# A two-layer encoder trunk on one core: folding neighbour blocks in mixer A, and moving q's transposes in mixer B

## The chip, the cores and the metric

The kernel runs on one core of a Trainium2 chip. The metric is the device time of one execution in microseconds (us). Five engines work side by side, each on its own list of instructions in order: TensorE (PE; its weight loads are PEld in the profile), VectorE (DVE), ScalarE (ACT), GpSimd (POOL) and SyncE (SP, which here only issues DMAs). TensorE writes to PSUM; the other memory on the core is SBUF.

## The reference

A sequence of 1024 tokens of width 1024, seen as a grid of 16 rows and 64 columns, goes through two layers. Layer 0 uses mixer A, layer 1 mixer B; each is followed by an output projection, a residual add and a gated embedding (`ple`).

```python
def mixer_a(h, w_in, rpb, w_out):          # 16 heads of 64
    q, k, v, gate = split(h @ w_in)
    # each query sees a clamped window of 8 rows x 16 columns of keys
    sc = einsum(q, k[window]) * scale + rpb[offset]
    o = einsum(softmax(sc), v[window])
    return (o * silu(gate)) @ w_out

def mixer_b(h, w_in, q_norm_g, k_norm_g, w_out):   # 16 q heads, 4 k/v heads
    q, k, v, gate = split(h @ w_in)
    q, k = rope(rms_norm(q)), rope(rms_norm(k))
    o = einsum(softmax(einsum(q, k) * scale), v)     # all 1024 keys
    return (o * silu(gate)) @ w_out

for i in range(2):
    x = x + mixer[i](rms_norm(x), ...)
    x = x + sigmoid(rms_norm(x) @ w_gate) * (p[i] @ w_proj)
return rms_norm(x)
```

All inputs are float32.

## The kernel before

**Tokens and blocks.** The tokens are laid out in 8 blocks of 128: block j holds the grid's columns 8j to 8j+7, all 16 rows. A window of 16 columns around a query of block j then lies in blocks j-1, j and j+1. Of block j-1 it takes the columns whose place in the block is at or after the query's, of block j+1 those before it. Blocks 0 and 7 are edges: the clamped window lies in two blocks there.

**Products.** Every float32 operand of a projection is split into a high and a low part (`HTh`/`HTl`, `wh`/`wl`, `PTh`/`PTl`), and the products are added up in PSUM. `mm` (line 317) issues every matmul of projections, scores and v products, so the profile tells these apart by tile names: `d` is a projection ("dense"), `s` scores, `o` products of probabilities with v, `t` transposes.

**Mixer A** (lines 655 to 998) goes through 128 steps (head h, block j). `f_S` computes the scores of one query block against its two or three key blocks (256 or 384 columns, L317 into `s`), and one DVE instruction (L754) adds the table `TB` of position biases and masks and takes the row minimum (the scores are negated). `f_E` (L763) is the exponential with its row sum. `f_T` transposes each block of 128 columns (L771), copies them to the high part (ACT, L774) and subtracts to get the low part (DVE, L775). `f_AV` multiplies one key block of v with the transposed probabilities of its two or three query blocks. `head_end` ends each half of a head: copy (L532), join (L496), reciprocals, and for each pair of heads the denominators go out to DRAM and come back spread over the partitions (`rb`, L503 and L505); then POOL multiplies `Y` by the gate `G` (L576) and by `rb` (L577), called four steps later. POOL also builds the table of the next head (`table`, L729, called at j = 1) and issues accumulating DMAs (L645, one a step while the list lasts).

**The order is written out by hand.** At step n of mixer A the program issues the small jobs (`head`), the transposes of step n, the exponential of step n+1, the scores of step n+2 and the v products of step n-2. `mix` strews the dense pieces (the next head's q and k, gates) between these items by weight. After each item `pulse` splits a weight unit when one is due and counts down the postponed pieces in `post`, so `QD = (2, 5, 8)` means that many items later.

**q and k of mixer A.** `qk_evac` takes a projected half head out of PSUM and makes `QS`, `KA` and `KB`, each with a part in both halves of the partitions: two ACT copies (L698, L699), two DVE subtractions (L702, L703), and two DVE copies of k's parts to the other half (L704, L707).

**Mixer B** (lines 1000 to 1326) runs 128 steps (head pair, half, head, 128 queries) in the same manner, with 1024 keys: scores into a two-bank PSUM tile (`psS`), minimum (L1211), exponential (L1217), eight transposes (`f_T`, L1227) into two buffers of `psT`, copies and subtractions (L1229, L1230), and `f_AV` for two query blocks at a time: eight products with the high part, then eight with the low. Once in 8 steps `q_stack` transposes the next q (L1181) into a `psT` buffer, and ACT copies it out (L1183). It stands in a queue called `after`, which `mix` runs behind the next dense piece. PSUM has eight banks: mixer B's pools are opened in the order `pd` (1), `psS` (4), `psT` (2), `psO` (1); the first projections alternate between `pd` and `psO`.

**The dense phases** (`dense_phase`, lines 1507 to 1729) follow each mixer. In the last one POOL multiplies X by the final norm's gain (L1706); the program puts these behind the test `n >= 17`, which counts dense pieces.

## Time and profile before

| | |
|---|---|
| median of 3 runs | 1526.33 us (1525.96 to 1526.63) |
| profiled execution, its own time | 1525.28 us |
| span of its profile | 1523.4 us |
| PE busy | 1496.9 us, 98% |
| DVE busy | 1096.4 us, 72% |
| ACT busy | 899.8 us, 59% |
| POOL busy | 303.8 us, 20% |
| attention loop of mixer A | about 57 to 530 us of the span |
| dense phase 0 | about 530 to 710 us |
| mixer B, start and loop | about 710 to 1338 us |
| dense phase 1 | about 1338 us to the end |

A row of the profile gives line, engine, operation, output<-inputs, sizes and count, then busy time in us, the mean of one in ns, and the idle time of the engine just before with what ended it. A row of a timeline gives start, duration, engine, line and operation; "x3" merges three in a row, and a bracket gives idle time before it and what ended that. The shown end of a matmul is modelled and overlaps the next one. Some matmul records are missing from the trace (352 transposes of L771 are shown, 368 are issued).

### The profile page before, as it was taken

What the parts mean: (1) busy time and instruction counts of PE and PEld (TensorE: products, weight loads), DVE (VectorE), ACT (ScalarE), POOL (GpSimd) and SP (SyncE); (2) the same over time, 40 slices, a digit from 0 to 9 for tenths busy, and PEclk for the clock granted to TensorE, in tenths of its full rate; (3) what the DMA queues carried; (4) which work ended last, traced back from release to release, by engine and by line L of the source; (5) the groups of instructions that cost most, each with busy time, mean ns of one, the idle gap of its engine ahead of it and who ended that gap; (6) DMA issues with size and microseconds to landing.
All of it is one profiled execution on the core that took longest, in us unless ns stands there. A gap on an engine that the chain in (4) does not pass through costs nothing.

```text
span 1523.4 us, 24376 instructions
## 1 busy us (share of the span) xinstructions
PE 1496.9 (98%) x8976; PEld 1314.9 (86%) x8976; DVE 1096.4 (72%) x2091; ACT 899.8 (59%) x1801; POOL 303.8 (20%) x413
## 2 busy tenths in 40 slices
PE   8999999999999999999999999999999999999997
PEld 8888988988988888888998999989999888878786
DVE  7566576377477599767888786777877777789856
ACT  6565465366466635443467776666767777744432
POOL 1222232133112000010222222443131300000022
PEclk9999999999999999999999999999999999999999
DMA  8325255263121963262210111111111122763123
GB/s 255 120 98 139 82 144 163 63 157 93 36 87 56 345 249 97 83 196 93 75 50 22 32 45 50 40 32 54 47 31 45 38 76 68 237 228 115 66 88 134
DMA packets 91096, 157.22 MB, mean 103 GB/s; under 512 B 18144, under 2 KB 54112, under 8 KB 90464
## 3 DMA queue, kind: packets, MB, share of 16 engines
q1 hardware_dynamic: 85824, 139.66, 27.9%
q0 software_dynamic: 2560, 8.39, 3.1%
q10 hardware_dynamic: 2592, 7.61, 1.4%
q8 instruction: 71, 1.16, 0.3%
q14 instruction: 49, 0.40, 0.1%
HBM read 125.10 MB, written 50.83 MB: 115 GB/s over the span
## 4 chain that ended last, share of the span: by engine, by line
PE 43%; DVE 6%; ACT 2%; issue 1%; DMA 0%; POOL 0%; ACTq 0%; DVEq 0%; POOLq 0%
PE d L317 19%; PE o L317 9%; PE s L317 7%; PE t L1227 7%; PE t L317 1%; DVE xn L1560 1%; DVE PTl L1230 1%; DVE X L1456 0%; PE t L1181 0%; DVE wl L231 0%; DVE mn L1211 0%; DVE HTl L482 0%; DVE HTl L1402 0%; ACT PTh L1229 0%; ACT th L1183 0%
## 5 line engine op out<-in xcount | busy, mean ns | idle before, releaser
L317 PE MATMUL d<-wh,HTh 128*128 128x256 f32 (+1 forms) x1032 | 342.5, 334 | 3.9 <-ACT HTh L481 1.6
L317 PE MATMUL d<-wh,HTl 128*128 128x256 f32 (+1 forms) x1032 | 338.0, 329 | 0.3 <-DVE HTl L482 0.3
L317 PE MATMUL d<-wl,HTh 128*128 128x256 f32 (+1 forms) x1032 | 336.7, 328 | 0.0
L1230 DVE TENSOR_TENSOR PTl<-t,PTh 128x512 fp32r<-128x512 f32 x256 | 165.1, 684 | 108.7 <-ACT PTh L1229 107.5
L317 PEld LDWEIGHTS d<-wh,HTh 128*128 128x128 f32 x1032 | 194.8, 190 | 24.5 <-ACT HTh L481 2.0
L317 PEld LDWEIGHTS d<-wl,HTh 128*128 128x128 f32 x1032 | 194.7, 190 | 19.3
L317 PEld LDWEIGHTS d<-wh,HTl 128*128 128x128 f32 x1032 | 194.9, 190 | 18.8 <-DVE HTl L482 0.5
L317 PE MATMUL d<-HTh,wh 128*128 128x512 f32 x504 | 205.2, 407 | 0.0
L317 PE MATMUL d<-HTh,wl 128*128 128x512 f32 x504 | 198.2, 393 | 0.0
L317 PE MATMUL d<-HTl,wh 128*128 128x512 f32 x504 | 197.3, 392 | 0.0
L1217 ACT ACTIVATE P<-s,mn 128x1024 f32<-128x1024 f32 x128 | 142.8, 1116 | 51.8 <-DVE mn L1211 50.9
L1229 ACT ACTIVATE PTh<-t 128x512 fp32r<-128x512 f32 x256 | 139.9, 594 | 52.8 <-PE t L1227 52.0
L1211 DVE TENSOR_REDUCE mn<-s 128x1 f32<-128x1024 f32 x128 | 154.7, 1209 | 11.2 <-PE s L317 11.0
L1227 PE MATMUL t<-ident,P 128*128 128x128 f32 x1024 | 136.4, 274 | 5.2 <-ACT th L1183 2.9
L317 PE MATMUL s<-KA,QS 128*128 128x512 f32 (+2 forms) x384 | 134.5, 404 | 0.0
L1227 PEld LDWEIGHTS t<-ident,P 128*128 128x128 f32 x1024 | 115.2, 140 | 16.6 <-DVE PTl L1230 6.7
L231 DVE TENSOR_TENSOR wl<-wstage,wh 128x1024 fp32r<-128x1024 f32 x78 | 100.3, 1290 | 34.9 <-ACT wh L226 34.4
L317 PE MATMUL s<-KB,QS 128*128 128x512 f32 (+2 forms) x384 | 121.6, 371 | 0.0
L775 DVE TENSOR_TENSOR PTl<-t,PTh 128x384 fp32r<-128x384 f32 (+1 forms) x128 | 66.6, 520 | 75.4 <-ACT PTh L774 74.0
L317 PE MATMUL o<-PTh,V 128*128 128x256 f32 (+2 forms) x672 | 118.5, 287 | 1.2 <-DVE Y L496 0.8
L317 PE MATMUL o<-PTl,V 128*128 128x256 f32 (+2 forms) x672 | 119.1, 288 | 0.7 <-DVE PTl L1230 0.6
L317 PEld LDWEIGHTS d<-HTh,wl 128*128 128x128 f32 x504 | 94.6, 188 | 21.7
(237 smaller groups left out, 2694.1 us busy)
## 6 DMA issues: line engine op xcount, KB each, us to landing
wstage<-in_wts SPq DMA_DIRECT2D x88, 512.0 KB
pp<-ppD SPq DMA_DIRECT2D x32, 256.0 KB
X<-in_x SPq DMA_DIRECT2D x15, 512.0 KB
rb<-rD SPq DMA_DIRECT2D x56, 128.0 KB
ppD<-th SPq DMA_DIRECT2D x20, 256.0 KB
tD0t<-in_wts SPq DMA_DIRECT2D x16, 256.0 KB
tD1t<-in_wts SPq DMA_DIRECT2D x16, 256.0 KB
xD<-X SPq DMA_DIRECT2D x8, 512.0 KB
```

The lines of the kernel that those rows point to most:

```text
L231: eng.tensor_tensor(lo[:, c:c + n], s[:, c:c + n], hi[:, c:c + n], ALU.subtract)
L317: pe.matmul(ps, a, b, start=first, stop=last, skip_group_check=True)
L775: dve.tensor_tensor(PTl[:, sl], ps[:, :m], PTh[:, sl], ALU.subtract)
L1211: dve.tensor_reduce(mn, ps, axis=AX.X, op=ALU.min)
L1217: act.activation(p, ps, AF.Exp, bias=mn, scale=-1.0, accum_out=RS[h, hf][:, t:t + 1])
L1227: pe.transpose(ps[:, i], p[:, k * 128:(k + 1) * 128], ident)
L1229: act.activation(PTh[:, ks, c], ps, AF.Copy)
L1230: dve.tensor_tensor(PTl[:, ks, c], ps, PTh[:, ks, c], ALU.subtract)
L1560: dve.scalar_tensor_tensor(xn, X[t], rn[m][:, i:i + 1], g1, op0=ALU.mult, op1=ALU.mult)
```

## The change

In mixer A, `f_S` still computes 384 columns for an inner step, and then a predicated DVE copy within PSUM puts the columns of block j+1 that the window takes into block j-1's place, over those that it doesn't take. The bias table is joined in the same way once a head (`join`). What follows, reduction, exponential, transposes, copies, runs on 256 columns in place of 384. After the transposes POOL parts the folded block again: it multiplies it by two 0/1 masks into the places of the two neighbours, once for `PTh` and once for `PTl`. The masks (`SIDE`) come by a DMA at the start. The exponential is issued two steps ahead, the scores three steps, and the v products come three steps behind. The two DVE copies of k become ACT copies, and the pieces of `qk_evac` have five places (`QD`). `Y` has a third buffer in layer 0.

In mixer B, `q_stack` is called inside `f_AV`, between the products with the high part and those with the low part. The `psS` pool is opened ahead of `pd`, and the first eight projection tiles come from `psS`. The test `n >= 17` becomes `not pend` (no transposes of the norm are left to issue).

```diff
+ENTRY = 8
-QD = (2, 5, 8)
+QD = (2, 4, 6, 7, 9)
+    sides = np.stack([c[:, None] >= c[None, :], c[:, None] < c[None, :], c[:, None] > c[None, :]], axis=1).astype(np.float32)
...
-    leave, after = Evac(), Evac()
-    after.wait = True
+    leave = Evac()
...
-            Y = sb.tile([128, 512], F32, name="Y", bufs=2)
+            Y = sb.tile([128, 512], F32, name="Y", bufs=3 if layer == 0 else 2)
...
-                    def two():
+                    def low_q():
                         dve.scalar_tensor_tensor(qs[hi, s], raw[lo], -0.125, qs[lo, s], op0=ALU.mult, op1=ALU.subtract)
+                    def low_k():
                         dve.tensor_tensor(kb[hi, s], raw[hi], ka[hi, s], ALU.subtract)
-                        dve.tensor_copy(ka[lo, s], ka[hi, s])
-                    def three():
-                        dve.tensor_copy(kb[lo, s], kb[hi, s])
+                    def across(k):
+                        act.activation(k[lo, s], k[hi, s], AF.Copy)
+                    parts = (one, low_q, lambda: across(ka), low_k, lambda: across(kb))
...
+            def join(h):
+                dve.copy_predicated(TB[h][:, 1], SIDE[:, 2].bitcast(mybir.dt.int32), TB[h][:, 3])
...
-                    tb = TB[h][:, 1:4]
-                sp = sb.tile([128, 384], F32, name="sp", bufs=3)
+                    tb = TB[h][:, 1:3]
+                    dve.copy_predicated(ps[:, 0:128], SIDE[:, 2].bitcast(mybir.dt.int32), ps[:, 256:384])
+                sp = sb.tile([128, 256], F32, name="sp", bufs=4)
...
-                for i in range(m):
-                    pe.transpose(ps[:, i], sp[:, i * 128:(i + 1) * 128], ident)
-                f0 = k0 * 3 + (j - k0 + 1)
-                sl = slice(f0, f0 + 2 * m - 1, 2)
-                act.activation(PTh[:, sl], ps[:, :m], AF.Copy)
-                dve.tensor_tensor(PTl[:, sl], ps[:, :m], PTh[:, sl], ALU.subtract)
+                inner = 0 < j < NT - 1
+                for i in range(2):
+                    c = 1 - i if inner else i
+                    pe.transpose(ps[:, i], sp[:, c * 128:(c + 1) * 128], ident)
+                k0 = near(j)[0]
+                f0 = 3 * j + 1 if inner else k0 * 3 + (j - k0 + 1)
+                f1 = 3 * NT + j % 2 if inner else f0 + 2
+                sl = slice(f0, f1 + 1, f1 - f0)
+                act.activation(PTh[:, sl], ps[:, :2], AF.Copy)
+                dve.tensor_tensor(PTl[:, sl], ps[:, :2], PTh[:, sl], ALU.subtract)
+                if inner:
+                    def apart():
+                        for pt in (PTh, PTl):
+                            pool.tensor_tensor(pt[:, 3 * j - 1:3 * j + 4:4], pt[:, f1:f1 + 1].to_broadcast([128, 2, 128]), SIDE[:, :2],
+                                               ALU.mult)
+                    apart()
...
             sync.dma_start(MK, mask)
+            sync.dma_start(SIDE, sides)
...
+                        if j == 5 and h + 1 < NH:
+                            join(h + 1)
-                    if n + 1 < len(steps):
-                        att.append((lambda n=n: f_E(*steps[n + 1]), CA[2]))
                     if n + 2 < len(steps):
-                        att.append((lambda n=n: f_S(*steps[n + 2]), CA[3]))
-                    if n >= 2:
-                        att += av_and_v(*steps[n - 2])
+                        att.append((lambda n=n: f_E(*steps[n + 2]), CA[2]))
+                    if n + 3 < len(steps):
+                        att.append((lambda n=n: f_S(*steps[n + 3]), CA[3]))
+                    if n >= 3:
+                        att += av_and_v(*steps[n - 3])
...
+            psS = es.enter_context(tc.tile_pool(name="bps", bufs=2, space=PSUM))
             pd = es.enter_context(tc.tile_pool(name="bpd", bufs=1, space=PSUM))
-            psS = es.enter_context(tc.tile_pool(name="bps", bufs=2, space=PSUM))
...
+                    if pro[1] <= ENTRY:
+                        return psS.tile([128, 1024], F32, name="s")[:, :512]
...
                 for k in range(NT):
                     mm(o, V[h // 4][:, k], PTh[:, k], t == 1 and k == 0, False)
+                while turned:
+                    turned.pop(0)()
                 for k in range(NT):
                     mm(o, V[h // 4][:, k], PTl[:, k], False, t == 3 and k == NT - 1)
...
-                        att.append((lambda hn=hn, fn=fn: after(lambda: q_stack(hn // 2, fn)), 0.0))
+                        att.append((lambda hn=hn, fn=fn: turned.append(lambda: q_stack(hn // 2, fn)), 0.0))
...
-                            while due and n >= 17:
+                            while due and not pend:
```

More of the change, by code (lines that the diff above doesn't have):

```diff
@@ L158, in trunk @@
 @with_exitstack
-def trunk(ctx, tc, x, wts, rpb, gains, hgains, mask, rope, gain0, out):
+def trunk(ctx, tc, x, wts, rpb, gains, hgains, mask, sides, rope, gain0, out):
     nc = tc.nc
@@ L664, in mixer_a @@
             MK = one.tile([128, 5, 128], F32, name="MK")
+            SIDE = one.tile([128, 3, 128], F32, name="SIDE")
             def dalloc():
@@ L933, in mixer_a @@
             ptp = es.enter_context(tc.tile_pool(name="ptp", bufs=1))
-            PTh = ptp.tile([128, NT * 3, 128], F32R, name="PTh")
-            PTl = ptp.tile([128, NT * 3, 128], F32R, name="PTl")
+            PTh = ptp.tile([128, NT * 3 + 2, 128], F32R, name="PTh")
+            PTl = ptp.tile([128, NT * 3 + 2, 128], F32R, name="PTl")
             for d in qk_items(0):
@@ L1024, in mixer_b @@
             later = Later()
+            turned = []
             pro = [False, 0]
             def qalloc():
-                pro[1] += 1
-                if pro[0] and pro[1] % 2 == 0:
-                    return psO.tile([128, 512], F32, name="o")[:, :256]
-                return pd.tile([128, 512], F32, name="d")[:, :256]
+                return dalloc()[:, :256]
             def rope_in(dst, raw, tab, eng):
```

30 lines of the change are left out of this document (14 added, 16 removed).

## The prediction

> **What bounds the kernel.** I read the page's engine table first, then busy time by stage, then TensorE's own timeline, then who waited for whom.
>
> ```profile
> PE 1496.9 (98%) x8976; PEld 1314.9 (86%) x8976; DVE 1096.4 (72%) x2091; ACT 899.8 (59%) x1801; POOL 303.8 (20%) x413
> PEclk9999999999999999999999999999999999999999
> ```
>
> ```profile
> 57.00:530.00 473.00, 471.33 (x2699) 411.40 (x2697) 297.58 (x672) 278.87 (x622) 106.57 (x131) 1.00 0.41 119
> 770.00:1338.00 568.00, 559.82 (x3835) 507.22 (x3835) 427.54 (x673) 404.48 (x751) 140.73 (x216) 1.00 0.19 58
> ```
>
> The second fence is busy time by stretch: start and end, length, then PE, weight loads, DVE, ACT and POOL, granted clock, DMA share and rate. The first row is mixer A's attention loop, the second mixer B's. TensorE is busy without a break in both, at a granted clock of 1.00. A matmul's shown duration overlaps the next one, so I price TensorE work by the distance from one start to the next, not by its bar.
>
> ```profile
> PE t L771 <- ACT sp L763: 1.0, 2, 0.8
> ...
> PE t L1227 <- ACT th L1183: 2.9, 7, 0.8
> ```
>
> ```profile
> PEld t L771 <- ACT sp L763: 6.7, 19, 1.1
> ...
> PEld t L1227 <- ACT th L1183: 4.5, 7, 1.0
> ```
>
> These are the waits (total us, times, longest) of matmuls and of weight loads. In mixer A the 1.0 us is the only wait of a matmul at all. So there only less TensorE work can buy time; in mixer B the largest wait is for the evacuation of q's transposes (L1183).
>
> **Mixer A, transposes.** Steps j = 1 to 6 of each head transpose two blocks in place of three: 16 x 6 = 96 transposes less.
>
> ```profile
> 521.19 0.49 PE L771 MATMUL t<-ident,sp 128*128 128x128 f32 x3
> 521.44 0.48 PE L317 MATMUL d<-wh,KA 128*128 128x512 f32 x1
> 521.76 0.40 PE L317 MATMUL d<-wl,KA 128*128 128x512 f32 x1
> 521.99 0.39 PE L317 MATMUL d<-wh,KB 128*128 128x512 f32 x1
> ...
> 523.37 0.38 PE L771 MATMUL t<-ident,sp 128*128 128x128 f32 x2
> 523.51 0.47 PE L317 MATMUL d<-wh,KA 128*128 128x512 f32 x1
> ```
>
> An inner step's three transposes take 521.44 - 521.19 = 0.25 us until the next matmul starts; the edge step, which has two already, 523.51 - 523.37 = 0.14. So a removed one is worth 0.11, and 96 x 0.11 = 10.6 us on the path. The first matmul behind transposes takes 521.76 - 521.44 = 0.32 where the next takes 0.23: each return from transposes costs 0.09, and in mixer A their number stays. The score products keep their 384 columns, so nothing else leaves TensorE.
>
> The Trainium skill ("TensorE: Matmul & The Clock Gate", Back-to-back issue gap) puts pairs of weight load and 128-column matmul at about 81 ns. By that the term would be an estimated 96 x 0.081 = 7.8 us, and the total 2.8 us later. The trace's 0.11 differs, and I take the trace.
>
> **Mixer A, the earlier exponential.** It is issued two steps ahead of its transposes in place of one; this should end the waits on L763. Bounds: 1.0 us (the matmuls' row) and 6.7 (the weight loads', part of which runs under the matmul before).
>
> ```profile
> 307.58 0.28 PE L317 MATMUL o<-PTl,V 128*128 128x256 f32 x1
> 308.00 0.55 PE L771 MATMUL t<-ident,sp 128*128 128x128 f32 x3
> ```
>
> Here a 256-column product is followed after 0.42 us; its kind takes 0.12 (the 0.97 us of eight, below), so 0.30 is lost though the matmul row books no wait. A handful of such cases beyond the 1.0 make about 2 us; I take 2.0, near the lower end.
>
> **Mixer A, DVE and ACT.**
>
> ```profile
> L754 DVE CUSTOM_DVE_ANT_0 sp<-s,tb 128x384 f32<-128x384 f32 x96 | 52.6, 548 | 10.8 <-PE s L317 10.5
> L754 DVE CUSTOM_DVE_ANT_1 sp<-s,tb 128x256 f32<-128x256 f32 x32 | 13.4, 419 | 0.8 <-PE s L317 0.3
> L775 DVE TENSOR_TENSOR PTl<-t,PTh 128x384 fp32r<-128x384 f32 x96 | 53.4, 556 | 64.6 <-ACT PTh L774 63.4
> L775 DVE TENSOR_TENSOR PTl<-t,PTh 128x256 fp32r<-128x256 f32 x32 | 13.2, 412 | 10.8 <-ACT PTh L774 10.6
> L774 ACT ACTIVATE PTh<-t 128x384 fp32r<-128x384 f32 x96 | 47.1, 490 | 56.4 <-PE t L771 55.5 <-issue 0.4
> L774 ACT ACTIVATE PTh<-t 128x256 fp32r<-128x256 f32 x32 | 12.2, 383 | 11.2 <-PE t L771 10.9
> L704 DVE CAST KA<-KA 64x512 fp32r<-64x512 f32 x32 | 15.2, 477 | 1.0
> L699 ACT ACTIVATE KA<-th 64x512 fp32r<-64x512 f32 x32 | 20.1, 629 | 0.6
> L1079 POOL TENSOR_TENSOR qt<-qt,ss 128x256 f32<-128x256 f32 x32 | 20.3, 663 | 34.4 <-DVE ss L336 28.9 <-DVE r L522 5.4
> L1048 POOL TENSOR_TENSOR qt<-qt,t 128x256 f32<-128x256 f32 x24 | 18.8, 784 | 1.9
> ```
>
> DVE loses 96 x (0.548 - 0.419) = 12.4 us at the reductions, 96 x (0.556 - 0.412) = 13.8 at the low parts, and 64 copies of k of the L704 kind, about 64 x 0.48 = 30. It gains 96 predicated copies and 16 joins of tables, 128x128 each, which the trace does not show. Below: 128 further columns in the reduction cost 0.13 us; above: the reduction of 256 columns, 0.42. I take 0.3: two operands in PSUM, but fewer columns than the upper row; 112 x 0.3 = 34. So DVE ends about 22 us lighter (bounds 9 and 42), of 298 in a 473 us stage. ACT loses 96 x (0.490 - 0.383) = 10 at the copies and as much at the exponentials, and gains 64 copies like L699, 64 x 0.63 = 40: +20 on 279. TensorE covers both, and no engine fills. Were that cover gone, a predicated copy would delay its scores by 0.13 to 0.42 us, at most 96 x 0.42 = 40 us in all; the cover is the score buffer, which has until two steps later (6 us, below) to be read. The scores start a step earlier, so a head's first find their q and k with less room: by the code the last copy of the half they read is issued at the end of step 3, and they come in step 5; a step is 3 us, the two copies on ACT 0.63 each, so I charge nothing. The pieces of v that follow each product in every fourth head come a step later with it; their tiles are read eight steps on.
>
> **Mixer A, POOL.** Two multiplications of 256 columns per inner step: 192 x 0.66 to 0.78, about 140 us, so 107 + 140 = 247 of 473. They are new on the way from transposes to the products with v: those now wait for POOL, and behind POOL's instruction stands its queue: table building (L729), the gate and denominator products (L576, L577), the accumulating DMAs.
>
> ```profile
> 223.51 0.33 PE L317 MATMUL o<-PTh,V 128*128 128x256 f32 x1
> 229.80 0.49 PE L771 MATMUL t<-ident,sp 128*128 128x128 f32 x3
> 233.50 0.49 PE L771 MATMUL t<-ident,sp 128*128 128x128 f32 x3
> 241.64 0.34 PE L317 MATMUL o<-PTh,V 128*128 128x384 f32 x1
> ```
>
> ```profile
> 233.46 1.29 POOL L577 TENSOR_TENSOR Y<-Y,rb 128x512 f32<-128x512 f32 x1 [5.79 <-DMA rb<-rD]
> ```
>
> With the products moved from two steps behind to three, the block transposed at 233.50 is read by the products two steps on, at about 241.64: 8.1 us, so a step is about 3. On the way stand transposes 0.14, copy 0.38, low part 0.41 and POOL 2 x 0.75: 2.4 us. That leaves 5.5 us for queues. The worst neighbour is the pair L576/L577, which waits for the denominators' DMA: products done at 223.51, DMA landed at 233.46. It is called four steps after those products, so POOL now reaches it behind the block of 229.80, at about 229.80 + 2.4 = 232.2, spends 1.3 on L576, and finds the DMA landed at 233.5. So the wait nearly goes; the pair holds the queue for 2.6. I charge 1 us of new waits (bounds 0 and the first rival's 41). A third Y buffer gives the pair room, and the extra table of 0/1 masks, one load of 196 KB during the start, I cost at nothing: it goes out ahead of the first table, and if that came late, by 1 us at most.
>
> **Mixer B, q's transposes.** Fifteen groups in the loop move from behind a dense piece into the middle of the v products.
>
> ```profile
> 1117.07 0.60 PE L1181 MATMUL t<-ident,qt 128*128 128x128 f32 x4
> 1117.51 0.60 PE L1227 MATMUL t<-ident,P 128*128 128x128 f32 x4
> 1118.64 0.66 PE L1227 MATMUL t<-ident,P 128*128 128x128 f32 x4 [0.54 <-ACT th L1183]
> ```
>
> ```profile
> 789.37 1.12 PE L317 MATMUL o<-PTl,V 128*128 128x256 f32 x8
> 790.34 1.04 PE L1227 MATMUL t<-ident,P 128*128 128x128 f32 x8
> 791.13 0.71 PE L317 MATMUL s<-KA,QS 128*128 128x512 f32 x2
> ```
>
> In the first fence P's second four transposes need the buffer that q's hold, and ACT has other work first. Four take 0.4 (eight: 791.13 - 790.34 = 0.79), so they start 1118.64 - 1117.51 - 0.4 = 0.73 late. Seven such waits: 2.9 us (matmuls' row) to 7 x 0.73 = 5.1; the weight loads' row says 4.5, and I take that. In the new place eight low products, 790.34 - 789.37 = 0.97 us, and the first four transposes stand in between, more than the wait lasted. Against it: in these seven cases q's transposes ran straight into P's, and now add a return, 7 x 0.09 = 0.6. Net 3.9. What hangs on them (two copies and two subtractions on ACT and DVE, no DMA) comes half a step later, and the scores that need it are five steps on.
>
> **Mixer B, PSUM order and the start.** The first eight tiles come from the score buffers, two as before.
>
> ```profile
> 715.65 0.39 PE L317 MATMUL d<-wh,HTh 128*128 128x256 f32 x1 [0.60 <-ACT th L1149]
> ```
>
> This third tile still waits for the first tile's evacuation. I take 0.2 gained (bounds -0.6 and +0.6). The changed test ahead of the last norm's gain products only moves when POOL gets them in its queue, which is otherwise empty there: nothing, +-0.5.
>
> **Sum.** -10.6 - 2.0 + 1.0 - 3.9 - 0.2 = -15.7. The profiled execution took 1525.28 us (span 1523.4 and 1.9 around it), so 1509.6; the median of the runs shown, 1526.33, lies 1.05 higher: 1510.6 in its terms.
>
> **Rivals.** (1) POOL sets mixer A's pace, the one on the slower side. Place: v products behind a multiplication held up by L577. It decides once POOL is delayed by more than the 5.5 us. If the DMA wait stays as it is (5.79 in the row) with 2.6 of work, that is 8.4 - 5.5 = 2.9 us for each of 14 pairs, 41 us: 1526.3 - 15.7 + 41 = 1552. Against it: the wait was long only because POOL arrived early. Chance 0.09.
> (2) Moving q's transposes does not help, because ACT still takes their evacuation late, behind an exponential; the wait only moves: -10.6 - 2.0 + 1.0 - 0.2 + 0.6 = -11.2, 1515.1. For it: ACT is 404 of 568 busy. Chance 0.14.
> (3) The waits were worth more: 6.7 for the exponentials, 5.1 for q, none for POOL: -10.6 - 6.7 - 4.5 - 0.2 = -22, 1504. Chance 0.12.
> (4) Mixer A's gain is eaten by small waits on POOL and the predicated copies, 0.11 per inner step being enough; what is left is mixer B: 1522 to 1526. Chance 0.10.
>
> **Numbers.** The forecast, 1507 to 1514, has 0.55. Below 0.2% (3 us) a measurement cannot tell a change. Faster: 0.55 + 0.14 + 0.12 and half of (4), 0.86; same 0.05; slower 0.09. The range 1504 to 1523 leaves out (1), half of (4) and the far part of (3).
>
> **What would show it.** L771 with 96 transposes less (272 by the code), in twos only; no wait of L771 on L763; new POOL rows of 0.7 us; no large wait of v products on POOL (otherwise rival 1, on the rows behind L577); the wait on L1183 gone (otherwise rival 2). A mean of the predicated copy above 1 us, or POOL's multiplications above 1.3, would make the prediction wrong.

## The result, and the profile after

The changed kernel takes 1517.28 us (median, 1515.82 to 1519.51) against 1526.13 for the kernel before on the same chip: ratio 0.9944, interval 0.9932 to 0.9957, which is 8.6 us less (the medians differ by 8.9). The forecast had been 15.7 us less; 1517.3 lies above the band of 1507 to 1514 that had the greatest chance, and inside the wider range of 1504 to 1523. The profiled execution was the fastest of the six, 1515.82 us with a span of 1514.0, 9.4 less than the profiled one before.

The line numbers moved a little: matmuls L317 are now L319, mixer A's transposes L771 are L776, its exponential L763 is L768, the reduction L754 is L760, the high and low parts L774/L775 are L781/L782, the denominators' products L576/L577 are L574/L575, mixer B's transposes L1227 are L1246 and q's L1181/L1183 are L1200/L1202. New are the predicated copy L757, the join of tables L736 and POOL's multiplications L786.

The page's engine table, then busy time by stretch (columns as before: PE, weight loads, DVE, ACT, POOL, clock, DMA):

```profile
PE 1483.9 (98%) x8880; PEld 1305.0 (86%) x8880; DVE 1087.9 (72%) x2139; ACT 917.5 (61%) x1865; POOL 450.8 (30%) x605
```

```profile
57.00:524.00 467.00, 461.84 (x2611) 403.36 (x2612) 289.39 (x720) 295.92 (x683) 253.79 (x323) 1.00 0.44 120
767.00:1330.00 563.00, 557.73 (x3835) 507.46 (x3833) 427.45 (x671) 404.08 (x751) 140.19 (x216) 1.00 0.19 58
```

TensorE has 96 matmuls less and is still 98% busy. In mixer A's loop DVE lost 8 us, ACT gained 17, POOL went from 107 to 254; no engine came near the stage's length.

Groups of instructions by line of the changed kernel: count, busy time, mean ns, idle before.

```profile
L776 PE MATMUL t<-ident,sp 128*128 128x128 f32 x256 | 49.0, 273 | 0.0
...
L757 DVE COPY_PREDICATED s<-SIDE,s 128x128 f32<-128x128 int32 x96 | 27.7, 288 | 18.6 <-PE s L319 17.8
...
L760 DVE CUSTOM_DVE_ANT_0 sp<-s,tb 128x256 f32<-128x256 f32 x96 | 40.7, 424 | 3.3
...
L786 POOL TENSOR_TENSOR PTl<-PTl,SIDE 128x256 fp32r<-128x256 f32 x96 | 89.7, 934 | 5.8 <-DVE PTl L782 5.7
L786 POOL TENSOR_TENSOR PTh<-PTh,SIDE 128x256 fp32r<-128x256 f32 x96 | 81.0, 844 | 197.1 <-ACT PTh L781 197.1
...
L736 DVE COPY_PREDICATED tb<-SIDE,tb 128x128 f32<-128x128 int32 x16 | 12.9, 807 | 0.1
```

The transposes come in twos only, 256 of them (352 before), and their matmuls never wait: the releaser sp L763 that L771 had is gone. (The 368 and 272 given above count 16 too many: 16 heads of six steps with three and two with two are 352, all in the trace, and 256 with twos only.) The predicated copy costs 0.288 us where I took 0.3; POOL's multiplications 0.84 and 0.93 where I took 0.66 to 0.78.

The waits (total us, times, longest) show what came instead, first of the changed kernel, then one row of the kernel before:

```profile
PE s L319 <- DVE mn L760: 2.8, 1, 2.8
...
PE d L319 <- ACT th L617: 2.1, 1, 2.1
...
PE o L319 <- POOL PTh L786: 1.1, 1, 1.1
...
POOL Y L575 <- DMA rb<-rD: 51.7, 12, 7.0
```

```profile
POOL Y L577 <- DMA rb<-rD: 142.4, 22, 8.9
```

The first three are the largest new waits of TensorE, each at one single place. The last two rows are forecast: POOL now reaches the denominators' products later and finds their DMA landed more often.

To see where each microsecond went I take the first or last row of a kind on TensorE's timeline as a milestone and compare the stretch between two milestones with the same stretch before. Differences in us:

| stretch on TensorE | after | start | tail | start_tail | b_only | q_only | old_lag | exp_late |
|---|---|---|---|---|---|---|---|---|
| up to the first score | +0.4 | 0.0 | +0.1 | +0.1 | +0.7 | -1.4 | 0.0 | +0.1 |
| to mixer A's first transposes | +3.4 | +0.4 | +5.0 | +0.4 | 0.0 | 0.0 | 0.0 | +0.4 |
| to its last transposes | -10.3 | -8.6 | -9.4 | -7.3 | -0.1 | -0.1 | +2.4 | -1.7 |
| to q's first transposes in mixer B (last head's end and a dense phase) | +3.1 | +3.1 | +0.7 | +0.4 | 0.0 | 0.0 | 0.0 | +0.2 |
| to mixer B's first transposes | +0.1 | 0.0 | 0.0 | 0.0 | 0.0 | 0.0 | -0.5 | 0.0 |
| to mixer B's last transposes | -5.1 | -5.0 | -5.0 | -5.0 | -5.1 | -4.8 | -5.1 | -5.2 |
| to its last matmul | -1.0 | -1.0 | -1.0 | -1.0 | -1.0 | 0.0 | -0.8 | -1.0 |
| all | -9.3 | -11.2 | -9.7 | -12.4 | -5.5 | -6.3 | -4.0 | -7.2 |

The other columns are experiments, below. The first row differs by up to 2 us between executions of kernels whose code is the same up to there, so I read single stretches, not the sums.

The changed kernel's column says it at once: the loop of mixer A and mixer B gave what was forecast and a bit more, and 6.5 us were lost at the two ends of mixer A, in stretches that I had costed at nothing (the start's part varies: the run tail, whose code is the same up to there, has +5.0). Here are the places, in the timeline of the changed kernel (start, length, engine, line). The start:

```profile
54.80 0.34 PE L319 MATMUL s<-KB,QS 128*128 128x384 f32 x1
...
56.60 0.83 DVE L704 TENSOR_TENSOR KB<-th,KA 64x512 fp32r<-64x512 f32 x1
57.46 0.42 DVE L760 CUSTOM_DVE_ANT_1 sp<-s,tb 128x256 f32<-128x256 f32 x1
...
57.95 0.45 PE L319 MATMUL s<-KA,QS 128*128 128x384 f32 x1 [2.81 <-DVE mn L760]
```

```profile
41.77 2.14 POOL L730 TENSOR_TENSOR tb<-MK,u 128x128 f32<-128x128 f32 x5 [4.10 <-DMA u<-U]
```

Scores now run three steps ahead, so a third score follows the first two at once. It needs the buffer that the first reduction reads. That reduction's table is long built (41.77 to 43.9), but on DVE it stands behind the subtractions of head 0's second half of q and k, the last of which, L704, ends at 57.43; the reduction begins 0.03 us later, at 57.46, and it does so right behind the last piece of k in every run. TensorE, with four dense pieces queued behind, stands for 2.8 us. The kernel before had the same late reduction (58.24, behind its L707) without a wait, because its third score came only at 61.6, behind the dense pieces.

The end of mixer A, one row of DVE after and its counterpart before:

```profile
526.06 0.69 DVE L547 TENSOR_TENSOR Y<-Y,rb 128x512 f32<-128x512 f32 x1 [2.90 <-ACT rb L516]
```

```profile
529.15 0.69 DVE L549 TENSOR_TENSOR Y<-Y,rb 128x512 f32<-128x512 f32 x1
```

With v products three steps behind, more of them lie behind the last transposes, and the last head's first half is summed up a step later: its normalisation (L513) begins 4.9 us behind the last transposes, where it was 2.4 before. DVE, which had gone straight on, waits 2.9 us. From there on the stretch is 2.6 us longer than before; the dense phase waits for DVE in several small pieces, 2.0 us by the matmuls' rows.

POOL, at the border of heads 8 and 9:

```profile
315.81 1.79 POOL L574 TENSOR_TENSOR Y<-Y,G 128x512 f32<-128x512 f32 x1
...
319.34 1.30 POOL L575 TENSOR_TENSOR Y<-Y,rb 128x512 f32<-128x512 f32 x1 [1.75 <-DMA rb<-rD]
319.38 1.81 DVE L591 SCALAR_TENSOR_TENSOR G<-th,G 128x512 f32<-128x512 f32 x1 [0.81 <-ACT th L587]
320.58 0.80 POOL L643 DMA_DIRECT2D tD1t<-in_wts  x1
321.13 0.99 POOL L786 TENSOR_TENSOR PTh<-PTh,SIDE 128x256 fp32r<-128x256 f32 x1
...
322.18 0.44 PE L319 MATMUL o<-PTh,V 128*128 128x384 f32 x1 [1.14 <-POOL PTh L786]
```

A gate product, the wait for the denominators, their product and the issue of a DMA stand in a row ahead of L786: rival 1's mechanism, but the wait on the DMA is 1.75 us and it delays TensorE at one place.

The last head's store:

```profile
486.96 7.01 SPq L211 DMA_DIRECT2D wstage<-in_wts  x3
494.14 0.33 SPq L618 DMA_DIRECT2D ppD<-th  x1
...
503.20 0.60 ACT L617 ACTIVATE th<-d 128x512 f32<-128x512 f32 x1 [5.12 <-DMA ppD<-th]
503.85 0.50 PE L319 MATMUL d<-wh,KA 128*128 128x512 f32 x1 [2.10 <-ACT th L617]
```

```profile
495.00:505.00 10.00, 7.91 (x39) 6.50 (x38) 3.02 (x11) 3.69 (x10) 2.29 (x4) 1.00 1.01 344
```

```profile
502.00:512.00 10.00, 10.00 (x54) 8.62 (x53) 3.89 (x12) 6.24 (x14) 0.00 (x0) 1.00 0.93 323
```

The last two fences are the ten microseconds behind this store after and before (before, it goes out at 502.17). ACT may write the buffer th again only when its store has landed, here 9.0 us after it went out; before, it wrote the buffer again 5.9 us after the store, without a wait for it. The DMA engines are full (1.01, 344 GB/s), but that alone is not it, for before they were nearly so (0.93, 323), and without a wait. What is new is the company: two loads of y now go out 0.6 and 0.2 us ahead of the store, where one went out 0.2 ahead and one 0.1 behind it, and two stores of y 0.4 and 0.9 us behind it, where they had gone 6.1 and 5.1 ahead. TensorE stands for 2.1 us. Nothing of this is in the forecast.

### The profile page after: what moved, and what is told of

Its sections match the earlier page's. It is cut to its first block, busy times and chain, and to the rows that moved or that the text cites. A ratio compares the mean times of both kernels' runs of the same rounds, so it can differ in the third digit from the quotient of the medians.

```text
span 1514.0 us, 24782 instructions
## 1 busy us (share of the span) xinstructions
PE 1483.9 (98%) x8880; PEld 1305.0 (86%) x8880; DVE 1087.9 (72%) x2139; ACT 917.5 (61%) x1865; POOL 450.8 (30%) x605
## 4 chain that ended last, share of the span: by engine, by line
PE 43%; DVE 6%; ACT 2%; issue 1%; DMA 0%; POOL 0%; ACTq 0%; DVEq 0%; POOLq 0%
PE d L319 19%; PE s L319 8%; PE o L319 8%; PE t L1246 7%; PE t L319 1%; DVE xn L1581 1%; DVE PTl L1249 1%; DVE X L1477 0%; DVE mn L1230 0%; PE t L1200 0%; DVE wl L233 0%; DVE HTl L480 0%; DVE HTl L1423 0%; ACT wh L228 0%; ACT P L1236 0%
## 5 line engine op out<-in xcount | busy, mean ns | idle before, releaser
L319 PE MATMUL d<-wh,HTh 128*128 128x256 f32 (+1 forms) x1000 | 332.9, 335 | 2.7 <-ACT HTh L479 1.7
L319 PE MATMUL d<-wh,HTl 128*128 128x256 f32 (+1 forms) x1000 | 328.9, 331 | 0.3 <-DVE HTl L480 0.3
L319 PE MATMUL d<-wl,HTh 128*128 128x256 f32 (+1 forms) x1000 | 327.9, 330 | 0.2 <-DVE wl L1375 0.2
L319 PEld LDWEIGHTS d<-wh,HTh 128*128 128x128 f32 x1000 | 188.5, 189 | 22.7 <-ACT HTh L479 2.0
L319 PEld LDWEIGHTS d<-wl,HTh 128*128 128x128 f32 x1000 | 188.5, 189 | 19.7 <-DVE wl L1375 0.6
L319 PEld LDWEIGHTS d<-wh,HTl 128*128 128x128 f32 x1000 | 188.8, 190 | 18.8 <-DVE HTl L480 0.5
L319 PE MATMUL d<-HTh,wh 128*128 128x512 f32 x504 | 204.7, 406 | 0.0
L319 PE MATMUL d<-HTh,wl 128*128 128x512 f32 x504 | 198.0, 393 | 0.0
L319 PE MATMUL d<-HTl,wh 128*128 128x512 f32 x504 | 197.4, 392 | 0.0
L786 POOL TENSOR_TENSOR PTh<-PTh,SIDE 128x256 fp32r<-128x256 f32 x96 | 81.0, 844 | 197.1 <-ACT PTh L781 197.1
L1246 PE MATMUL t<-ident,P 128*128 128x128 f32 x1024 | 134.8, 273 | 2.6 <-DVE PTl L1249 2.0
L319 PE MATMUL s<-KA,QS 128*128 128x512 f32 (+2 forms) x384 | 134.2, 404 | 2.8 <-DVE mn L760 2.8
L1246 PEld LDWEIGHTS t<-ident,P 128*128 128x128 f32 x1024 | 115.5, 140 | 12.8 <-DVE PTl L1249 6.9
L319 PE MATMUL s<-KB,QS 128*128 128x512 f32 (+2 forms) x384 | 121.4, 370 | 0.0
L319 PE MATMUL o<-PTl,V 128*128 128x256 f32 (+2 forms) x672 | 120.1, 290 | 1.1 <-DVE PTl L1249 0.6
L319 PE MATMUL o<-PTh,V 128*128 128x256 f32 (+2 forms) x672 | 118.4, 287 | 2.4 <-POOL PTh L786 1.1
L319 PEld LDWEIGHTS d<-HTh,wl 128*128 128x128 f32 x504 | 94.6, 188 | 21.7
```

The source lines that it names most:

```text
L319: pe.matmul(ps, a, b, start=first, stop=last, skip_group_check=True)
L786: pool.tensor_tensor(pt[:, 3 * j - 1:3 * j + 4:4], pt[:, f1:f1 + 1].to_broadcast([128, 2, 128]), SIDE[:, :2], ALU.mult)
L1246: pe.transpose(ps[:, i], p[:, k * 128:(k + 1) * 128], ident)
```

## The experiments

My theory after the comparison was: the fold and mixer B are worth what was forecast; the longer lags (scores three ahead, products three behind) cost 2.9 us at the start and 2.2 at the end of mixer A, and late POOL and the store take 2 us each. Rivals: the waits just move; or the longer lags are worth nothing and should be taken back. Each ratio is to the kernel before on the same chip.

| run | ratio (interval) | median, us |
|---|---|---|
| changed kernel | 0.9944 (0.9932 to 0.9957) | 1517.28 |
| start | 0.9925 (0.9911 to 0.9938) | 1513.94 |
| tail | 0.9940 (0.9927 to 0.9952) | 1515.41 |
| start_tail | 0.9910 (0.9897 to 0.9924) | 1510.8 |
| b_only | 0.9960 (0.9948 to 0.9972) | 1518.38 |
| q_only | 0.9966 (0.9953 to 0.9978) | 1519.71 |
| old_lag | 0.9966 (0.9953 to 0.9978) | 1520.11 |
| exp_late | 0.9950 (0.9937 to 0.9964) | 1517.59 |
| pool_twice | 1.0241 (1.0220 to 1.0262) | 1562.03 |
| fin_later | 0.9910 (0.9895 to 0.9925) | 1511.11 |
| loads_later | 0.9907 (0.9893 to 0.9922) | 1510.42 |
| both_later | 0.9907 (0.9893 to 0.9920) | 1511.3 |
| pool_half | 0.9923 (0.9911 to 0.9936) | 1513.23 |

**start: the third score behind the leading dense pieces.**

```diff
-            f_S(0, 2)
...
+                if h == 0:
+                    att.insert(0, (lambda: f_S(0, 2), CA[3]))
```

> The changed kernel with one thing moved: the third score product of the start (head 0, block 2) is issued behind the four leading dense pieces, not ahead of them. Theory (the start costs: the third score waits for the first one's buffer, which the first reduction reads late because the first table is late): the 2.8 us wait of s on the reduction goes and the kernel gains 2.5 to 3.2 us on the changed one, about 1514.5. Rival (the wait stands beside another one, for the first table itself, and the transposes behind it wait instead): under 0.8 us gained, 1516.5 or more.

The wait is gone and 2.9 us come back (0.9944 - 0.9925 = 0.0019 of 1525; the intervals overlap a little, and the two profiles differ by 1.8). The reason that the expectation gives for the late reduction, a late first table, is not what the trace shows: the reduction follows L704 here too. Its waits:

```profile
PE o L319 <- POOL PTh L786: 2.2, 2, 1.7
...
PE d L319 <- ACT th L617: 1.8, 1, 1.8
...
PE s L319 <- DVE mn L760: 0.2, 1, 0.2
```

The wait on L760 fell from 2.8 to 0.2, but the one on POOL doubled: part of what is won early is given back there, at heads 8 and 9 for the most part.

**tail: from the last steps on, v products two steps behind again.**

```diff
-                    if n >= 3:
+                    if 3 <= n <= 125:
                         att += av_and_v(*steps[n - 3])
+                    if n >= 125:
+                        att += av_and_v(*steps[n - 2])
...
-range(NT - 3, NT)
+range(NT - 2, NT)
```

> The changed kernel, but from step 125 of mixer A on the v products come two steps behind, not three, as before the change. Theory (the tail costs: head 15's first half ends a step later, VectorE waits 2.9 us for its denominators and reaches the next phase's sums 2.75 us later against TensorE, which then waits 2.2 us in dense phase 0): those waits go, 1.8 to 2.6 us gained, about 1515. Rival (VectorE is as late as that because the dense pieces and stores of the last head are late, whatever the half's end): under 0.7 us.

```profile
525.21 0.69 DVE L547 TENSOR_TENSOR Y<-Y,rb 128x512 f32<-128x512 f32 x1
```

This is L547 of tail's timeline: it no longer waits, and the stretch behind mixer A loses 0.7 us in place of 3.1. The whole gained only 0.0004, 0.6 us, within the intervals: in its profile the first transposes came 1.5 us later than in the changed kernel, whose code is the same up to there, and its loop gave 0.9 less (four products, 0.6 us, moved back ahead of its last transposes). So the place is shown and its worth, alone, is not.

**start_tail: both.**

> Both of these moves in the changed kernel. Theory (two separate places): the gains add, 4.3 to 5.8 us, about 1512.3, that is 0.991 of the kernel before. Rival (slack behind mixer A takes up what its start gains): not more than the larger one alone, 1514.5.

0.9910, 5.2 us less than the changed kernel (0.0034 of 1525); as expected and a little better. This settles the two ends: 5.2 us of the 7.1 that were missing. The parts, 2.9 and 0.6, add up to less than the whole, but their intervals are each some 2 us wide to either side. In the table's stretches the two ends give back 5.7 us, and the loop loses 3.0 of them again (-7.3 for -10.3, with the 0.6 of the four products), so the profiles differ by 3.1 only; the changed kernel's is the fastest of its executions, this one the slowest of its own.

**b_only: the kernel before with mixer B's part alone.**

```diff
-                        att.append((lambda ...: after(lambda: q_stack(hn // 2, fn)), 0.0))
+                        att.append((lambda ...: turned.append(lambda: q_stack(hn // 2, fn)), 0.0))
...
+                while turned:
+                    turned.pop(0)()
...
+                    if pro[1] <= 8:
+                        return psS.tile([128, 1024], F32, name="s")[:, :512]
```

> The kernel before with mixer B's part alone (q's transposes inside the v products, the PSUM order, the first tiles from the score buffers); mixer A as before. Theory: 5.1 us from the loop and 1.0 behind it, as the two traces differ there, less 0.3 at the entry: 5.8 us faster than before, 0.9962. The prediction had 4.1 us, 0.9973. Rival (part of mixer B's gain in the trace came from mixer A's weights and DMAs standing elsewhere): 3 us or less.

0.9960, 6.1 us, near the theory's 5.8. This run leaves the test `n >= 17` as it was and has the same 1.0 us behind the loop as the changed kernel, so the new test is worth nothing that shows.

**q_only: of that, the moved transposes alone; the order of PSUM tiles as before.**

> The kernel before with q's transposes of mixer B moved into the v products, and nothing else; the order of the PSUM tiles at mixer B's start stays as before. b_only, with both, gave 0.996: -5.1 us in mixer B's loop, -1.0 behind it (a wait of 0.7 us on L619 gone), +0.3 at its start. Theory: all of the loop's gain is the moved transposes', and the order of tiles brings nothing: about 1518.5, 0.996, loop -5.1. Rival: the order of tiles also ends the wait behind the loop: loop -5.1, behind it 0, so 1519.5, 0.9967. Second rival, the prediction's size: loop -3.9.

```profile
PE d L317 <- ACT th L619: 0.7, 1, 0.7
```

This row of q_only's waits is that of the kernel before; in b_only it is gone. By the stretches the transposes bring 4.8 in the loop, the order of the tiles 0.3 there and 1.0 behind it, by ending this wait, which no step of mine had. So the expectation's rival is what happened: the order of the tiles ends the wait behind the loop. The times agree (0.9966 against 0.9960), though their intervals overlap. The prediction's rival 2, that moving q's transposes does not help, falls with the 4.8.

**old_lag: the fold kept, mixer A's old order of steps.**

```diff
-            f_E(0, 1)
-            f_S(0, 2)
...
-                        att.append((lambda n=n: f_E(*steps[n + 2]), CA[2]))
-                        att.append((lambda n=n: f_S(*steps[n + 3]), CA[3]))
-                        att += av_and_v(*steps[n - 3])
+                        att.append((lambda n=n: f_E(*steps[n + 1]), CA[2]))
+                        att.append((lambda n=n: f_S(*steps[n + 2]), CA[3]))
+                        att += av_and_v(*steps[n - 2])
```

> The changed kernel with mixer A's old order of steps: scores two steps ahead, exponential one step ahead, v products two steps behind; the fold of blocks, POOL's multiplications and mixer B's part stay. It tells what the longer lags are worth beside the fold. Theory: the lags cost 2.9 us at the start and 2.2 behind the last head, which come back here, but the room for POOL falls from 5.5 us to 2.5, so v products wait for POOL whenever the denominators' pair stands ahead in its queue (about once a head, 0.5 to 2 us), and the waits for the exponential, about 2 us, come back: 1520 to 1545, waits of v products on POOL of 8 to 30 us. Rival: the lags buy nothing, POOL's 2.4 us of path fit in two steps: 1511 to 1515, waits on POOL under 3 us.

```profile
PE o L319 <- POOL PTl L786: 5.6, 9, 1.0
...
PE o L319 <- POOL PTh L786: 3.0, 4, 1.3
...
PE t L776 <- ACT sp L768: 2.1, 5, 1.0
```

0.9966: what is left is no more than mixer B's part alone gives (0.9960, the intervals overlap). Both ends of mixer A are as before (0.0), so the longer lags are what costs there; but the loop, with 96 transposes less, is 2.4 us longer than before. The rows above have 8.6 us of waits on POOL and 2.1 on the exponential. With two steps' room the fold gains nothing; with three the loop gains 7 to 10. The rival falls.

**exp_late: in start_tail, the exponential back to one step ahead.**

```diff
-            f_E(0, 1)
...
-                        att.append((lambda n=n: f_E(*steps[n + 2]), CA[2]))
+                        att.append((lambda n=n: f_E(*steps[n + 1]), CA[2]))
```

> Base: the run start_tail (1510.8 us, 0.991). Only the exponential of mixer A is put back to one step ahead of its transposes; scores stay three steps ahead, v products three behind. It prices the prediction's term of 2.0 us for the earlier exponential. The prediction's step: waits of the transposes on L768 come back, 1.0 us by the matmuls' row and about 2 in all: 1512.8, 0.9923. Rival a: the earlier scores alone had ended these waits; no row of L776 on L768, 1510.5 to 1511.5. Rival b: the waits are worth what the weight loads' row said, 6.7 us: 1517.5, 0.9954.

```profile
PEld t L776 <- ACT sp L768: 12.2, 16, 1.5
...
PE t L776 <- ACT sp L768: 4.3, 9, 1.0
```

0.9950, 6.1 us more than start_tail (0.0040): rival b in size. Against the kernel before (rows 1.0 and 6.7) these waits are larger. It is not the reduction or its predicated copy that holds the exponential: scores are three steps ahead here, and every exponential begins at least 1.5 us behind its reduction. ACT's own queue stands ahead of it, at the largest wait with these rows:

```profile
313.12 0.62 ACT L697 ACTIVATE QS<-th 64x512 fp32r<-64x512 f32 x1
313.75 0.63 ACT L698 ACTIVATE KA<-th 64x512 fp32r<-64x512 f32 x1
314.40 0.38 ACT L781 ACTIVATE PTh<-t 128x256 fp32r<-128x256 f32 x1
314.81 0.51 ACT L768 ACTIVATE sp<-sp,mn 128x256 f32<-128x256 f32 x1
```

The transposes start at 315.47, 1.46 us late by the weight loads' row. The term of 2.0 priced the waits that were there before, and not those of the new order. Not all of the 6.1 are waits on the exponential: a wait of 2.8 us on another evacuation (tb, L617) stands in this run's rows too, where start_tail has 0.4.

**pool_twice: in the changed kernel, each multiplication of L786 twice.**

```diff
-                        for pt in (PTh, PTl):
+                        for pt in (PTh, PTl, PTh, PTl):
```

> The changed kernel with each of POOL's block multiplications done a second time into the same place (192 more of them, 0.84 to 0.93 us each, about 171 us): the output is not the reference's, only the time is read. It moves POOL from about 254 us of 473 in mixer A's loop to 425 and an inner step's pair from 1.8 to 3.55 us, over a step's 3 us. It tests the point from which POOL decides (in the prediction: a delay of more than 5.5 us between a block's transposes and its products). Theory: within each head the queue falls behind by 0.5 us per inner step, on top of about 4.2 us of path and 2.6 us of denominators' products, so the slack is used up at the end of each head and TensorE waits for POOL 1 to 4 us a head: 1533 to 1580. Rival: the slack of three steps hides it too, POOL makes up the delay at the two edge steps of each head: within 3 us of the changed kernel, 1514 to 1520.

(The second product writes the same values again, so nothing of the computation changes, other than the expectation says.)

```profile
57.00:524.00 467.00, 437.27 (x2386) 375.42 (x2387) 295.67 (x662) 266.98 (x619) 373.20 (x474) 0.98 0.36 94
```

```profile
PE o L319 <- POOL PTh L786: 15.4, 12, 3.1
PE o L319 <- POOL PTl L786: 8.2, 22, 1.1
```

1562 us, 45 more than the changed kernel (0.0297). POOL is at 373 of 467, 80%, and the products with v wait for it in 34 places. So the step from 54% to 80% busy lies across the point from which POOL decides in this order. The rows of the matmuls have 23.6 us of waits on POOL, those of the weight loads 35.5; the granted clock in this stretch is 0.98 in place of 1.00, which I estimate at up to 9 us of the 45 (2% of 467). That 45 is near rival 1's 41 is chance: rival 1 priced waits of POOL for a DMA, and here POOL is full of work. A step is 3.5 us long in the changed kernel (452 us between its first and last transposes, 128 steps), not the 3 of the prediction and of this expectation.

**fin_later, loads_later, both_later: in start_tail, the denominators' products, the last loads of y, or both, a step later.**

```diff
-FIN = (4, 4)
+FIN = (5, 4)
...
-YLOAD_A, YLOAD_B = 0, 118
+YLOAD_A, YLOAD_B = 1, 118
```

> Base: the run start_tail (1510.8 us, 0.991), which still waits 1.7 us for POOL's product around t = 320. Here mixer A's gate and denominator products (L574, L575) and the accumulating DMAs are called one step, about 3 us, later than there; nothing else differs. Theory: POOL stands at L575 waiting for the denominators' DMA (51.7 us in 12 waits in the changed kernel) and the block's product behind it comes late; called later, it finds the DMA landed. Then the wait of 1.7 us goes: about 1509, ratio 0.990. Rival: POOL's own work at that place is too long (a gate product of up to 1.3 us, a table and an issue of a DMA in a row), whatever L575 waits for: the wait stays above 1 us and the time within 0.5 us of start_tail. A third possibility: products called later make the sums of the last heads later and cost at the end of mixer A up to 2 us: 1511 to 1513.

> Base: the run start_tail (1510.8 us, 0.991). Here the loads of y for each pair of heads in mixer A are issued one step, about 3 us, later; nothing else differs. In the changed kernel the last pair's store of k's and p's partials is issued beside three weight tiles, the load of y and two stores, the DMA share is 0.93 to 1.08 for 10 us, and TensorE waits 2.1 us for the evacuation (ACT L617) behind it; 1.5 us in start_tail. Theory: the bytes of y are what the store shares the queues with, so with them out of the way the wait falls under 0.5 us: about 1509.5, ratio 0.990. Rival: the store is late because it stands in the queue of SP behind the weight tiles, whose buffers come free late: the wait stays at 1.2 us or more, the time within 0.5 us of start_tail.

> Base: the run start_tail (1510.8 us, 0.991). Here the denominators' products are called a step later (as in the run fin_later, 0.991, whose wait of TensorE on POOL of 1.7 us was gone while that on ACT L617 had grown from 1.5 to 2.2) and the last loads of y a step later (as in the run loads_later, 0.9907, whose wait on L617 was gone while that on POOL had grown from 1.7 to 2.2). Theory: each wait was taken up by the other because the last head's store lands at a time of its own; with both out of the way, 1.7 + 1.5 = 3 us are free: about 1508, ratio 0.989, neither wait above 0.5 us. Rival: the time is then held by a third wait (the high parts of the norm's transposes, HTh L479, 1.8 us in the base, or DVE's weight splitting in the last head): 1510 to 1511.5.

Rows of the waits of fin_later and of loads_later, and the largest wait of mixer A that is left in both_later:

```profile
PE d L319 <- ACT th L617: 2.2, 1, 2.2
```

```profile
PE o L319 <- POOL PTh L786: 2.2, 1, 2.2
```

```profile
PE t L776 <- DVE PTl L782: 2.1, 2, 1.1
```

Each edit ends the row that it aims at: fin_later has no row of v products on POOL (1.7 in start_tail), loads_later none on th of L617 (1.5). So it matters when each is issued. (By the code the first edit moves the two products alone and not the accumulating DMAs, and the second the loads of the last head alone, other than their expectations say.) But in fin_later the store's wait grew, in loads_later POOL's, and fin_later and both_later wait 2.1 us for the low parts, 1.1 at each of two places. The trace of fin_later shows why, at the second of them:

```profile
314.02 3.33 DVE L572 TENSOR_TENSOR Y<-Y,rb 128x512 fp32r<-128x512 f32 x1
```

In start_tail this instruction took 0.68. Here it stands beside POOL's work, which goes on until 316.79; it ends 0.56 later, DVE's low parts come late behind it, and TensorE waits for them at 318.67. So the wait on POOL was not ended but came by another way. What loads_later and both_later win in the loop is in part lost in the dense phase behind it: their stretches to q's first transposes are +1.6 and +2.0, where start_tail has +0.4. The profile of both_later has the shortest span, 1507.1, of which 1.5 us is a start before the first score that was shorter by chance; its times, 1508.88 to 1512.15, are those of start_tail (0.9907 against 0.9910). The expected 3 us are not in them: a miss. What is left of the difference between the profiles stays open; both_later's is the fastest of its four executions and start_tail's the slowest.

**pool_half: in start_tail, the low parts' multiplication on DVE.**

```diff
-                        for pt in (PTh, PTl):
-                            pool.tensor_tensor(pt...
+                        for eng, pt in ((pool, PTh), (dve, PTl)):
+                            eng.tensor_tensor(pt...
```

> Base: the run start_tail (1510.8 us, 0.991). Only the second multiplication of each inner step (the low parts') goes to DVE, 96 of them; POOL keeps the high parts'. POOL's share of the path from transposes to products falls from 1.6 to about 0.8 us and its busy time in mixer A by about 85; DVE gains 96 products of 256 columns at about 0.4 us (the low parts' subtraction of that size takes 0.42): 38 us. Theory: POOL's queue is what costs at heads 8 and 9 (wait of 1.7 us, 3 in all there), and DVE has room: 1508.5, 0.9895, no wait on POOL above 0.5. Rival: DVE now comes late for reductions and evacuations in front of TensorE, 0.1 us or more per inner step: 1515 to 1525.

```profile
L786 DVE TENSOR_TENSOR PTl<-PTl,SIDE 128x256 fp32r<-128x256 f32 x96 | 56.9, 593 | 3.3
```

```profile
PE s L319 <- DVE mn L760: 2.7, 5, 0.7
```

0.9923, about 2 us more than start_tail, within the intervals. No wait on POOL is left, but DVE takes 0.593 us where I had 0.4 from the subtraction out of PSUM (0.425 for the 17 that met no work of POOL, 0.63 for the 79 that did), and scores now wait for the reduction behind it. The wait moved to another engine.

The best of the versions are start_tail and the three edits of calls and loads on it, 0.991: about 5 us less than the changed kernel, and not told apart from each other.

## Why the prediction was right in direction and 7 us off in size

- **The path was read rightly.** TensorE bounded both mixers, at a clock of 1.00, and the step that pays is the one that takes work from it. Added up by distances from start to start, the transposes take 17.8 us where they took 28.9: 11.1 less, 0.116 each, forecast 10.6. By the 81 ns that the Trainium skill states ("TensorE: Matmul & The Clock Gate", Back-to-back issue gap) it would have been an estimated 7.8; the measurement bears out the row of this kernel instead.
- **The steps that failed are the ones costed at nothing.** "A head's first scores find q and k with less room ... I charge nothing" and "the extra table ... by 1 us at most" looked at the right place for the wrong thing: the scores did not wait for q, k or the masks but for the score buffer, held by a reduction that stands on DVE behind k's subtraction. I had named that buffer as the cover ("until two steps later") and not asked whether it covers in the first steps, when three scores come at once and DVE still works on head 0's k. And of the products three steps behind I priced only the room they give, not that the last head has one more step of them behind its last transposes, with DVE and a dense phase hanging on it. The trace before had both: its first scores at 54 us with the reduction at 58.24, and L549 of DVE following without a wait. start_tail shows 5.2 us.
- **POOL.** Forecast 1.0 of new waits; the matmuls' row has 1.1, the weight loads' rows 2.0 for the high parts and 1.0 for the low. The mechanism was right, the place as well (the pair L574/L575 with its DMA), and the multiplications were under-sized by a fifth (0.89 for 0.75). DVE came out 8 us lighter in the loop, not 22 (the joins of tables took 12.9 for 4.8, and the subtractions of q and k, L701 and L704, 5.5 more than before, 0.80 and 0.87 us each for 0.73 and 0.75), and as no engine came near its bound, that cost nothing.
- **The earlier exponential.** The waits on it are gone, as forecast. Its worth in the new order is at most 6.1 us (exp_late), three times the 2.0; part of that is a loss it prevents, so it does not come on top of the 9.4.
- **The store of the last head's partials, 2.1 us, was in no step.** At that point the kernel runs 8.0 us early (the store goes out at 494.14 for 502.17), and y's stores only 1.6 and 2.0 (494.52 and 495.04 for 496.12 and 497.06), so they meet. loads_later shows that without y's loads beside it the store lands in time; it shows no gain, and the stores alone were not moved.
- **Mixer B: -6.1 for -4.1.** The transposes gave 4.8 for 3.9, and the order of tiles 1.3 for 0.2, by a wait behind the loop (L619) that I had not connected with it. At mixer B's start, where the 0.2 was forecast, the stretch brought nothing (0.0 to +0.1): its wait for the evacuation is 0.9 us for 0.6. So this term came out larger for another reason than mine.

Sum, by terms: -11.1 for the transposes, about -2 for the waits on the exponential, -6.1 for mixer B, and +1.1 to +3.0 (POOL, by the matmuls' row or the weight loads'), +2.1 (store), +5.2 (both ends): -10.8 to -8.9, where the times say -8.6 and the profile -9.4. That the total is more than half of the forecast is in part luck: mixer B gave 2.0 more than forecast, while of the 11.6 us forecast for mixer A about 8.6 - 6.1 = 2.5 remained (3.4 by the profile's stretches). Rival 4 (small waits eat mixer A's gain) was nearest to what happened in mixer A, but with a few large waits, most of them at its ends, and none per step.

## What to carry to other kernels

When work is issued further ahead or further behind, price the two ends of the loop as well as the middle: at the start the deeper order asks for buffers before anything has released one, at the end it leaves one more step of work behind the last input; both can be taken back by giving the first and the last steps the short order. A fold that takes work from the bound engine and hands it to idle ones pays only if the order gives those engines the time, so the two belong in one estimate. A wait that an edit ends can come back by another engine or in a later stage; so measure the time, and not only the wait.

## What the runs showed of the hardware

- The same predicated copy of 128x128 took 0.288 us in PSUM (L757) and 0.807 in SBUF (L736), where single ones lay between 0.30 and 1.61 us. Told apart by the trace: the three of L736 during which POOL computed nothing took 0.30, the other 13 on average 0.92. The multiplication of pool_half (L786 on DVE, from SBUF) does the same, 0.425 in 17 without POOL and 0.63 in 79 with it, and so do the subtractions of k (L704), 0.689 in four and 0.89 in 28. Out of PSUM there is no such difference: L782 took 0.42 either way, L757 0.29. So it is POOL's work beside them, and not operands in SBUF as such, that makes them long.
- DVE's L591 took 1.81 us at 319.38, begun 0.04 after POOL's L575, and ended at 321.19, 0.55 after POOL had; its mean is 0.773. The Trainium skill ("SBUF — State Buffer", SBUF: two separate sides) describes the ports that DVE with two SBUF operands and GpSimd share as an exclusive lock, held for a whole instruction. This row agrees with it, as do the numbers above.
- In fin_later, where POOL's multiplications and DMA issues followed one another without a break, L572 of DVE took 3.33 us in place of 0.68 and ended 0.56 after the last of them: it lost not one instruction of POOL but a row of them. No wait is booked for it; the instruction's own time grows.
